# Relative-position softmax: whole-head partitions and chunks of five and six rows in place of one-row tiles

## The chip, the cores and the metric

The kernel runs on one core of a Trainium2 chip. The metric is device time in microseconds (us) of one execution; the time before is a median of 1363.56 us over four runs. The core has a vector engine (DVE), a scalar engine for exponentials (ACT), a general engine that also issues DMAs (GpSimd, called POOL in the profile) and a queue engine (SyncE, SP). Sixteen DMA engines move data between the chip's memory (HBM) and the on-chip memory (SBUF, 128 partitions). The tensor engine isn't used.

## What is computed

Logits of shape 2 x 8 x 2112 x 2112 in float32 get a bias that depends on the head and on the clipped distance between row and column, and then a softmax over the last axis:

```python
B, H, S, _ = logits.shape            # 2, 8, 2112
max_rel = 16
pos = np.arange(S)
rel = pos[:, None] - pos[None, :]
rel_clipped = np.clip(rel, -max_rel, max_rel) + max_rel
bias = rel_bias[:, rel_clipped].copy()        # rel_bias: 8 x 33
logits = logits + bias[None, :, :, :]
logits = logits - logits.max(axis=-1, keepdims=True)
exp = np.exp(logits)
return (exp / exp.sum(axis=-1, keepdims=True)).astype(np.float32)
```

So in each row the bias is one constant to the left of a band of 33 columns around the diagonal, another constant to the right of it, and 33 different values in the band. Input and output are 285.48 MB each; every element is read once and written once. Neither kernel subtracts the row's maximum, which a softmax doesn't need as long as the exponentials stay in range.

## The kernel before

The 33,792 rows of all heads are cut into 264 tiles of 128 consecutive rows; partition p of a tile holds one row of 8448 bytes. A pool `io` of 20 buffers holds the tiles `L`. Per tile:

- SyncE issues the load (line 110).
- DVE adds the band from a template, over 160 columns around the diagonal (line 136). The templates `T` (one per head) and `TP` (for tiles that cross from one head into the next) are made at the start: an extended bias row `e8` is written to a scratch tensor `eD` in HBM, read back shifted by one column per partition (line 65) and copied in reverse order (line 73).
- ACT computes the exponentials in place and sums them, in two instructions where the row has columns to the right of the band: line 143 for the columns up to the band's end, with the left constant as its bias operand, and line 151 for the rest, with the right constant. Templates hold the difference to the left constant. Each has an accumulator read behind it.
- DVE adds the two sums (line 162), takes the reciprocal (line 163) and multiplies the tile by it in place (line 165).
- GpSimd issues the store (line 167).

Loads thus stand on SyncE's queue, with the template loads among the first of them, and stores on GpSimd's. The tile framework allots buffers, places the waits and fixes each engine's order when the program is built; the engines work through their own orders and meet at semaphores. A load that reuses a buffer waits for the store of the tile 20 earlier. On SyncE, a wait for an earlier load on the same semaphore is also placed.

Of the kernel before, what the change touches and what calls it, by code (L numbers as in the profile page):

```python
# [1 line left out]

# [4 lines left out]

FP32 = mybir.dt.float32
EXP = mybir.ActivationFunctionType.Exp  # L10
ADD = mybir.AluOpType.add


@with_exitstack
def kernel(
    ctx: ExitStack,
    tc: tile.TileContext,
    logits: bass.AP,
    rel_bias: bass.AP,
    out: bass.AP,  # L20
):
    nc = tc.nc
    P = 128
    B, H, S, S2 = logits.shape
    assert S == S2
    MR = 16
    W = 2 * MR + 1
    BAND = P + 2 * MR
    EXT = P - 1
    ELEN = 2 * EXT + W  # L30

    logits_f = logits.flatten_outer_dims()
    out_f = out.flatten_outer_dims()
    NR = B * H * S
    assert NR % P == 0
    NT = NR // P

    const = ctx.enter_context(tc.tile_pool(name="const", bufs=1))
    dram = ctx.enter_context(tc.tile_pool(name="dram", bufs=1, space=bass.MemoryType.DRAM))

    rb8 = const.tile([H, W], FP32, tag="rb8")
    nc.sync.dma_start(out=rb8, in_=rel_bias)
    rbB = const.tile([P, H, W], FP32, tag="rbB")
    nc.sync.dma_start(
        out=rbB,
        in_=bass.AP(tensor=rel_bias.tensor, offset=rel_bias.offset, ap=[[0, P], [1, H * W]]),
    )

    e8 = const.tile([H, ELEN], FP32, tag="e8")
    nc.vector.tensor_copy(out=e8[:, 0:EXT], in_=rb8[:, 0:1].to_broadcast([H, EXT]))  # L50
    nc.vector.tensor_copy(out=e8[:, EXT : EXT + W], in_=rb8[:, :])  # L51
    nc.vector.tensor_scalar(  # L52
        out=e8[:, 0 : EXT + W],
        in0=e8[:, 0 : EXT + W],
        scalar1=rb8[:, W - 1 : W],
        scalar2=None,
        op0=mybir.AluOpType.subtract,
    )
    nc.vector.memset(e8[:, EXT + W :], 0.0)  # L59
    eD = dram.tile([H, ELEN], FP32, tag="eD")  # L60
    nc.sync.dma_start(out=eD, in_=e8)

    def load_template(t, p0, np_, h):
        x = const.tile([P, BAND], FP32, tag="X", name="X", bufs=4)
        nc.sync.dma_start(
            out=x[p0 : p0 + np_],
            in_=bass.AP(
                tensor=eD.tensor,
                offset=eD.offset + h * ELEN,
                ap=[[1, np_], [1, BAND]],  # L70
            ),
        )
        nc.vector.tensor_copy(  # L73
            out=t[p0 : p0 + np_],
            in_=bass.AP(
                tensor=x.tensor,
                offset=x.offset + p0 * list(x.ap[0])[0] + (BAND - 1),
                ap=[[list(x.ap[0])[0], np_], [-1, BAND]],
            ),
        )  # L80

    T = []
    for h in range(H):
        t = const.tile([P, BAND], FP32, tag=f"T{h}", name="T")
        load_template(t, 0, P, h)
        T.append(t)
    TP = []
    for k in range(H // 2):
        t = const.tile([P, BAND], FP32, tag=f"TP{k}", name="TP")
        load_template(t, 0, 64, 2 * k)  # L90
        load_template(t, 64, 64, 2 * k + 1)
        TP.append(t)
    io = ctx.enter_context(tc.tile_pool(name="io", bufs=20))
    small = ctx.enter_context(tc.tile_pool(name="small", bufs=16))

    def rb_at(h, k, p0, p1):
        return rbB[p0:p1, h, k : k + 1]

    for t in range(NT):
        rs = P * t  # L100
        f0 = rs // S
        f1 = (rs + P - 1) // S
        if f0 == f1:
            segs = [(0, P, f0, rs - f0 * S)]
        else:
            split = f1 * S - rs
            segs = [(0, split, f0, rs - f0 * S), (split, P, f1, 0)]

        L = io.tile([P, S], FP32, tag="L")
        nc.sync.dma_start(out=L, in_=logits_f[rs : rs + P, :])  # L110

        def seg_ab(p0, p1, i0):
            n = p1 - p0
            c0 = i0 - MR
            return c0, max(c0, 0), min(i0 + n + MR, S)

        max_slots = 1
        for (p0, p1, f, i0) in segs:
            _, _, b = seg_ab(p0, p1, i0)
            max_slots = max(max_slots, 1 + (b < S))  # L120

        s = None
        if max_slots == 2:
            s = small.tile([P, 2], FP32, tag="s", name="s")
        tot = small.tile([P, 1], FP32, tag="tot")

        for (p0, p1, f, i0) in segs:
            h = f % H
            n = p1 - p0
            c0, a, b = seg_ab(p0, p1, i0)  # L130
            nslots = 1 + (b < S)
            if len(segs) == 1:
                tmpl = T[h]
            else:
                tmpl = TP[(f0 % H) // 2]
            nc.vector.tensor_tensor(  # L136
                out=L[p0:p1, a:b],
                in0=L[p0:p1, a:b],
                in1=tmpl[p0 : p0 + n, a - c0 : b - c0],
                op=ADD,  # L140
            )
            acc0 = s[p0:p1, 0:1] if max_slots == 2 else tot[p0:p1, 0:1]
            nc.scalar.activation(  # L143
                out=L[p0:p1, 0:b],
                in_=L[p0:p1, 0:b],
                func=EXP,
                bias=rb_at(h, W - 1, p0, p1),
                accum_out=acc0,
            )
            if nslots == 2:  # L150
                nc.scalar.activation(  # L151
                    out=L[p0:p1, b:S],
                    in_=L[p0:p1, b:S],
                    func=EXP,
                    bias=rb_at(h, 0, p0, p1),
                    accum_out=s[p0:p1, 1:2],
                )
            elif max_slots == 2:
                nc.vector.memset(s[p0:p1, 1:2], 0.0)  # L159

        if max_slots == 2:
            nc.vector.tensor_tensor(out=tot, in0=s[:, 0:1], in1=s[:, 1:2], op=ADD)  # L162
        nc.vector.reciprocal(out=tot, in_=tot)  # L163

        nc.vector.tensor_scalar_mul(out=L[:], in0=L[:], scalar1=tot[:])  # L165

        nc.gpsimd.dma_start(out=out_f[rs : rs + P, :], in_=L[:])  # L167


# [1 line left out]
_INS = ['logits', 'rel_bias']  # L171
_OUTS = [((2, 8, 2112, 2112), 'float32')]


# [23 lines left out]
```

The softmax here doesn't subtract the row's maximum and nothing guards it: scores larger than these inputs give would overflow.

## Time and profile before

| | us |
|---|---|
| median of four runs | 1363.56 (1362.77 to 1364.3) |
| the profiled execution, its time | 1364.13 |
| the profiled execution, its span | 1362.0 |
| ACT busy | 657.5 |
| DVE busy | 518.5 |
| DVE multiply over 128x2112 (line 165), one | 1.320 |
| ACT exponential over 128x2112 (line 143), one | 2.054 |
| accumulator read behind it, one | 0.186 |
| DVE band add over 128x160 (line 136), one | 0.325 |
| DVE reciprocal (line 163), one | 0.164 |
| issue of one store on GpSimd (line 167) | 0.532 |

The span runs from the first to the last event that the profiler recorded; the time of the same execution is 2.1 us more. Busy shares are averages over the whole span. Idle time of an engine costs nothing where another resource sets the pace; which one does is read from the slices, the chain of work that ended last, and the waits. The slices cut the span into 40 equal parts, with a digit for the busy tenths of the mean DMA engine and, below, the GB/s moved.

### The profile page before, as it was taken

What the parts mean: (1) busy time and instruction counts of PE and PEld (TensorE: products, weight loads), DVE (VectorE), ACT (ScalarE), POOL (GpSimd) and SP (SyncE); (2) the same over time, 40 slices, a digit from 0 to 9 for tenths busy, and PEclk for the clock granted to TensorE, in tenths of its full rate; (3) what the DMA queues carried; (4) which work ended last, traced back from release to release, by engine and by line L of the source; (5) the groups of instructions that cost most, each with busy time, mean ns of one, the idle gap of its engine ahead of it and who ended that gap; (6) DMA issues with size and microseconds to landing.
All of it is one profiled execution on the core that took longest, in us unless ns stands there. A gap on an engine that the chain in (4) does not pass through costs nothing.

```text
span 1362.0 us, 3994 instructions
## 1 busy us (share of the span) xinstructions
DVE 518.5 (38%) x1084; ACT 657.5 (48%) x1057; POOL 140.6 (10%) x268
## 2 busy tenths in 40 slices
DVE  3434343343334333334343333433433433333432
ACT  3454444544445444454444544445444454444543
POOL 0011011010101110111011010111101101101100
DMA  8999999999999999999999999999999999999996
GB/s 292 413 428 428 427 427 428 428 426 427 428 428 426 427 428 428 426 427 429 427 426 428 428 427 426 428 428 427 426 428 428 427 426 428 428 427 426 428 428 286
DMA packets 78030, 572.36 MB, mean 420 GB/s; under 512 B 8744, under 2 KB 10416, under 8 KB 10416
## 3 DMA queue, kind: packets, MB, share of 16 engines
q1 hardware_dynamic: 39984, 286.62, 50.3%
q0 software_dynamic: 38016, 285.49, 49.7%
q14 instruction: 30, 0.25, 0.0%
HBM read 286.59 MB, written 285.48 MB: 420 GB/s over the span
## 4 chain that ended last, share of the span: by engine, by line
DMA 98%; issue 1%; DVE 0%; ACT 0%; SPq 0%; POOLq 0%; POOL 0%; ACTq 0%; DVEq 0%
DMA L<-in_logits_dram 96%; DMA X<-eD 1%; DMA eD<-e 0%; ACT L L143 0%; SPq L110 0%; DMA rb<-in_rel_bias_dram 0%; DVE L L165 0%; DVE T L73 0%; POOLq L193 0%; DVE tot L162 0%; POOL out_dram L167 0%; ACT L L151 0%; DVE tot L163 0%; DVE L L136 0%; DVE e L52 0%
## 5 line engine op out<-in xcount | busy, mean ns | idle before, releaser
L151 ACT ACTIVATE L<-L,rbB 128x1968 f32<-128x1968 f32 (+31 forms) x256 | 297.1, 1160 | 655.9 <-DMA L<-in_logits_dram 619.8
L165 DVE TENSOR_SCALAR L<-L,tot 128x2112 f32<-128x2112 f32 x264 | 348.5, 1320 | 8.4
L143 ACT ACTIVATE L<-L,rbB 128x144 f32<-128x144 f32 (+33 forms) x272 | 333.2, 1225 | 29.2 <-DVE L L136 23.8
L167 POOL DMA_DIRECT2D out_dram<-L x264 | 140.4, 532 | 1213.1 <-DVE L L165 1055.3
L136 DVE TENSOR_TENSOR L<-L,T 128x160 f32<-128x160 f32 (+1 forms) x256 | 82.9, 324 | 350.0 <-DMA L<-in_logits_dram 334.6
L162 DVE TENSOR_TENSOR tot<-s 128x1 f32<-128x1 f32 x256 | 40.7, 159 | 423.1 <-ACT L L143 422.5
L163 DVE RECIPROCAL tot<-tot 128x1 f32<-128x1 f32 x264 | 43.3, 164 | 26.3 <-ACT L L143 17.7
L143 ACT ACTIVATION_READ_ACCUMULATOR L<-L,rbB 128x1 f32 (+1 forms) x272 | 50.7, 186 | 0.0
L151 ACT ACTIVATION_READ_ACCUMULATOR L<-L,rbB 128x1 f32 (+1 forms) x256 | 47.6, 186 | 0.0
L136 DVE TENSOR_TENSOR L<-L,TP 64x80 f32<-64x80 f32 x16 | 3.8, 236 | 7.9 <-DMA L<-in_logits_dram 7.7
L73 DVE COPY T<-X 128x160 f32<-128x160 f32 x8 | 1.6, 236 | 12.1 <-DMA X<-eD 12.1
L151 ACT ACT_TABLE_LOAD x1 | 1.3, 1283 | 8.9 <-DMA L<-in_logits_dram 8.9
L73 DVE COPY TP<-X 64x160 f32<-64x160 f32 x8 | 1.9, 238 | 4.7 <-DMA X<-eD 4.6
L50 DVE COPY e<-rb 8x127 f32<-8x127 f32 x1 | 0.2, 213 | 1.2 <-DMA rb<-in_rel_bias_dram 1.2
L59 DVE MEMSET e<- 8x127 f32 x1 | 0.2, 164 | 0.8 <-PEq L182 0.8
L159 DVE MEMSET s<- 64x1 f32 x8 | 0.5, 59 | 0.0
L52 DVE TENSOR_SCALAR e<-e,rb 8x160 f32<-8x160 f32 x1 | 0.3, 292 | 0.0
L51 DVE COPY e<-rb 8x33 f32<-8x33 f32 x1 | 0.2, 160 | 0.0
L182 POOL MEMSET const-float32-0.0<- 128x1 f32 x1 | 0.1, 98 | 0.2 <-issue 0.2
L182 POOL MEMSET const-bfloat16-1.0<- 128x1 bf16 x1 | 0.1, 101 | 0.0
L182 POOL MEMSET const-float32-1.0<- 128x1 f32 x1 | 0.1, 98 | 0.0
L182 POOL MEMSET const-uint8-127<- 128x1 uint8 x1 | 0.1, 98 | 0.0
## 6 DMA issues: line engine op xcount, KB each, us to landing
L<-in_logits_dram SPq DMA_DIRECT2D x264, 1056.0 KB, 40.5
out_dram<-L POOLq DMA_DIRECT2D x264, 1056.0 KB, 13.5
X<-eD SPq DMA_DIRECT2D x8, 80.0 KB, 4.2
X<-eD SPq DMA_DIRECT2D x8, 40.0 KB, 7.6
rbB<-in_rel_bias_dram SPq DMA_DIRECT2D x1, 132.0 KB, 5.2
rb<-in_rel_bias_dram SPq DMA_DIRECT2D x1, 1.0 KB
eD<-e SPq DMA_DIRECT2D x1, 9.0 KB
```

The lines of the kernel that those rows point to most:

```text
L50: nc.vector.tensor_copy(out=e8[:, 0:EXT], in_=rb8[:, 0:1].to_broadcast([H, EXT]))
L52: nc.vector.tensor_scalar(out=e8[:, 0 : EXT + W], in0=e8[:, 0 : EXT + W], scalar1=rb8[:, W - 1 : W], scalar2=None, op0=mybir.AluOpType.sub ...
L73: nc.vector.tensor_copy(out=t[p0 : p0 + np_], in_=bass.AP(tensor=x.tensor, offset=x.offset + p0 * list(x.ap[0])[0] + (BAND - 1), ap=[[list ...
L136: nc.vector.tensor_tensor(out=L[p0:p1, a:b], in0=L[p0:p1, a:b], in1=tmpl[p0 : p0 + n, a - c0 : b - c0], op=ADD,)
L143: nc.scalar.activation(out=L[p0:p1, 0:b], in_=L[p0:p1, 0:b], func=EXP, bias=rb_at(h, W - 1, p0, p1), accum_out=acc0,)
L151: nc.scalar.activation(out=L[p0:p1, b:S], in_=L[p0:p1, b:S], func=EXP, bias=rb_at(h, 0, p0, p1), accum_out=s[p0:p1, 1:2],)
L159: nc.vector.memset(s[p0:p1, 1:2], 0.0)
L162: nc.vector.tensor_tensor(out=tot, in0=s[:, 0:1], in1=s[:, 1:2], op=ADD)
L163: nc.vector.reciprocal(out=tot, in_=tot)
L165: nc.vector.tensor_scalar_mul(out=L[:], in0=L[:], scalar1=tot[:])
L167: nc.gpsimd.dma_start(out=out_f[rs : rs + P, :], in_=L[:])
L182: nc = _bacc.Bacc("TRN2", target_bir_lowering=False, num_devices=1)
```

## The change

Rows are dealt out differently. Two heads have 4224 rows, which is 128 x 33: partition p now owns 33 consecutive rows of a pair of heads, partitions 0 to 63 those of the first head and 64 to 127 those of the second. A chunk takes rows j to j + r of each partition's 33, so in HBM it is one contiguous run of r x 8448 bytes per partition. Chunks alternate between 5 and 6 rows, with smaller ones (1, 2, 4, 6, 4, 6, 4, 6) in the first pair and (5, 6, 5, 6, 4, 3, 2, 1, 1) in the last; there are 53 in all. Buffers are two of 5 rows and two of 6. The first four loads are issued on SyncE ahead of everything else there, the other 49 on GpSimd; all stores are issued on SyncE. A load waits until the store four chunks earlier has landed.

The bias is no longer a band: for each of the four pairs of heads a strip `F` of 2144 columns is built on DVE, in one buffer, from the bias values and from masks that an iota on GpSimd helps to make. Row j of a chunk uses the strip shifted by j columns, so one DVE addition covers up to three whole rows (line 148, over 128x6336). ACT then takes one exponential per row over all 2112 columns with its sum (line 152), DVE one reciprocal for up to three rows (line 153) and one multiply per row (line 156). Templates, scratch tensor and the additions of two partial sums are gone.

In the built program DVE doesn't finish one chunk before the next: for most pairs of chunks the order is both additions of a 6-row chunk, reciprocal and multiplies of its first half, the first addition of the 5-row chunk, then the second half of the 6-row chunk, and so on.

```diff
-    io = ctx.enter_context(tc.tile_pool(name="io", bufs=20))
-    small = ctx.enter_context(tc.tile_pool(name="small", bufs=16))
+    NB = S // W
+    R = 3
+    SLOT = (5, 6)
+    FW = S + W - 1
+    fpool = ctx.enter_context(tc.tile_pool(name="fpool", bufs=1))
+    io = ctx.enter_context(tc.tile_pool(name="io", bufs=2))
+    small = ctx.enter_context(tc.tile_pool(name="small", bufs=8))
+    chunks = []
+    for k in range(H // 2):
+        for b in range(B):
+            sizes = [5, 6] * 3
+            if not chunks:
+                sizes = [1, 2, 4, 6, 4, 6, 4, 6]
+            if k == H // 2 - 1 and b == B - 1:
+                sizes = [5, 6, 5, 6, 4, 3, 2, 1, 1]
+            j = 0
+            for r in sizes:
+                chunks.append((k, (b * H + 2 * k) * S, j, r))
+                j += r
+    def rows(t, row, j, r):
+        return bass.AP(
+            tensor=t.tensor,
+            offset=t.offset + (row + j) * S,
+            ap=[[W * S, P], [1, r * S]],
+        )
+    def load(n, eng):
+        k, row, j, r = chunks[n]
+        size = SLOT[n % 2]
+        L = io.tile([P, size * S], FP32, tag=f"L{size}", name="L")
+        eng.dma_start(out=L[:, 0 : r * S], in_=rows(logits, row, j, r))
+        return L
+    rbB = const.tile([P, H // 2, 2, W], FP32, tag="rbB")
+    nc.scalar.dma_start(
...
+    NPRE = 4
+    pre = [load(n, nc.sync) for n in range(NPRE)]
+    qm = const.tile([P, NB], FP32, tag="qm")
+    for p0 in (0, NB):
+        nc.gpsimd.iota(
+            qm[p0 : p0 + NB],
...
+    for m, op in ((eq, ALU.is_equal), (lt, ALU.is_gt), (gt, ALU.is_lt)):
+        nc.vector.tensor_scalar(out=m, in0=qm, scalar1=0.0, scalar2=None, op0=op)
...
+    def bias_rows(k):
+        F = fpool.tile([P, FW], FP32, tag="F", name="F")
+        low = rbP[:, k, W - 1 : W]
+        high = rbP[:, k, 0:1]
+        rest = small.tile([P, NB], FP32, tag="rest", name="rest", bufs=2)
+        nc.vector.tensor_scalar(out=rest, in0=lt, scalar1=low, scalar2=None, op0=ALU.mult)
+        nc.vector.scalar_tensor_tensor(
+            out=rest, in0=gt, scalar=high, in1=rest, op0=ALU.mult, op1=ALU.add
+        )
...
+        nc.vector.tensor_tensor(out=blocks, in0=wide(eq), in1=rev, op=ALU.mult)
+        nc.vector.tensor_tensor(out=blocks, in0=blocks, in1=wide(rest), op=ALU.add)
+        nc.vector.tensor_copy(out=F[:, 0:MR], in_=low.to_broadcast([P, MR]))
+        nc.vector.tensor_copy(out=F[:, FW - MR : FW], in_=high.to_broadcast([P, MR]))
+        return F
-    for t in range(NT):
...
-        L = io.tile([P, S], FP32, tag="L")
-        nc.sync.dma_start(out=L, in_=logits_f[rs : rs + P, :])
...
-        nc.gpsimd.dma_start(out=out_f[rs : rs + P, :], in_=L[:])
+    F, fk = None, None
+    for n, c in enumerate(chunks):
+        k, row, j, r = c
+        if k != fk:
+            F, fk = bias_rows(k), k
+        L = pre[n] if n < NPRE else load(n, nc.gpsimd)
+        pitch = list(L.ap[0])[0]
+        for s0 in range(0, r, R):
+            w = min(R, r - s0)
+            L3 = bass.AP(
+                tensor=L.tensor, offset=L.offset + s0 * S, ap=[[pitch, P], [S, w], [1, S]]
+            )
+            F3 = bass.AP(
+                tensor=F.tensor,
+                offset=F.offset + W - 1 - j - s0,
+                ap=[[list(F.ap[0])[0], P], [-1, w], [1, S]],
+            )
+            nc.vector.tensor_tensor(out=L3, in0=L3, in1=F3, op=ALU.add)
+            tot = small.tile([P, R], FP32, tag="tot", name="tot")
+            for i in range(w):
+                x = L[:, (s0 + i) * S : (s0 + i + 1) * S]
+                nc.scalar.activation(out=x, in_=x, func=EXP, accum_out=tot[:, i : i + 1])
+            nc.vector.reciprocal(out=tot[:, 0:w], in_=tot[:, 0:w])
+            for i in range(w):
+                x = L[:, (s0 + i) * S : (s0 + i + 1) * S]
+                nc.vector.tensor_scalar_mul(out=x, in0=x, scalar1=tot[:, i : i + 1])
+        nc.sync.dma_start(out=rows(out, row, j, r), in_=L[:, 0 : r * S])
```

## The prediction

> **What bounds the kernel now.** I read the busy table first, then the slices, the chain, the queue table, the waits of the queue that issues the loads, and last the head and the tail in windows.
>
> ```profile
> span 1362.0 us, 3994 instructions
> ...
> DVE 518.5 (38%) x1084; ACT 657.5 (48%) x1057; POOL 140.6 (10%) x268
> ...
> DMA  8999999999999999999999999999999999999996
> GB/s 292 413 428 428 427 427 428 428 426 427 428 428 426 427 428 428 426 427 429 427 426 428 428 427 426 428 428 427 426 428 428 427 426 428 428 427 426 428 428 286
> ...
> q1 hardware_dynamic: 39984, 286.62, 50.3%
> q0 software_dynamic: 38016, 285.49, 49.7%
> ...
> DMA 98%; issue 1%; DVE 0%; ACT 0%; SPq 0%; POOLq 0%; POOL 0%; ACTq 0%; DVEq 0%
> ```
>
> No engine is half busy; the DMA engines are full in 38 of 40 slices, and 98% of the chain is DMA. The two queues' packet times add up to 100% of 16 engines' span. So two things matter: the plateau of 426 to 429 GB/s, and the two slices at the ends.
>
> ```profile
> SPq L110 <- DMA L<-in_logits_dram: 1153.4, 252, 5.4
> ...
> 0.00:20.00 20.00, 6.04 (x20) 8.56 (x13) 1.40 (x6) 1.00 0.78 230
> 20.00:40.00 20.00, 7.82 (x22) 7.28 (x12) 1.59 (x3) 1.00 0.97 370
> ...
> 200.00:600.00 400.00, 152.43 (x317) 196.29 (x315) 41.45 (x78) 1.00 1.01 427
> 600.00:1000.00 400.00, 154.07 (x318) 196.78 (x320) 41.44 (x79) 1.00 1.01 428
> ...
> 1340.00:1350.00 10.00, 3.83 (x8) 4.38 (x7) 1.06 (x2) 1.00 0.61 253
> 1350.00:1356.00 6.00, 1.48 (x2) 1.55 (x2) 0.53 (x1) 1.00 0.73 300
> 1356.00:1362.00 6.00, 0.00 (x0) 0.00 (x0) 0.00 (x0) 1.00 0.18 75
> ```
>
> The first line: each load waits for an earlier load, not for a buffer. The windows (length, busy of DVE, ACT, POOL, clock, DMA share, GB/s) show the plateau and its ends. At 427.5 GB/s (427 from 200 to 600 us, 428 from 600 to 1000) the page's 572.36 MB take 1338.9 us, so 23.1 us of the span are lost: at the head 20 x (1 - 230/427.5) + 20 x (1 - 370/427.5) = 11.9, the remaining 11.2 at the tail.
>
> **What the skill says.** "DMA: Bandwidth & Descriptors", Where 436 GB/s comes from: the ceiling is 16 ports x 32 B x 850 MHz = 435.2 GB/s. Same page, Why small descriptors are slow: some 3 cycles per packet plus 32 B of descriptor data. A row of 8448 B is 264 beats; with 3 + 1 cycles the estimate is 435.2 x 264/268 = 428.7, and the plateau is 427.5: the trace agrees. Same page, Why a DMA increments its semaphore by 16 and not by 1: one descriptor moves one contiguous run of the last dimension. The trace agrees for rows: 33,792 per queue, and with one completion entry for each of the 16 engines per DMA that makes 264 x (128 + 16) = 38,016 packets, as q0 has; longer runs it doesn't show. "SBUF — State Buffer", Who interferes with whom: DVE in a two-port mode, as an fp32 tensor_scalar is, shuts GpSimd out while an instruction lasts, and so its descriptor writing; the trace before can't show it, since each GpSimd DMA there follows the DVE multiply. "VectorE: DVE Perf Modes", The TRN2 errata: an fp32 tensor_tensor takes (N + 151)/0.96 ns; for 160 that is 324, and the band add measured 325.
>
> **The change, part by part.**
>
> *Transfer rate.* Loads and stores go from 128 runs of 8448 B to 128 runs of 5 or 6 rows (42 to 51 KB). If a run stays one packet, the four cycles are paid once for 5.5 rows: 1452 beats + 4, and one cycle more for a share of the completion entry (one per engine and DMA, beside eight data packets), so 435.2 x 1452/1457 = 433.7 GB/s (estimate from the page, fitted to the plateau). Bounds: 427.5 (runs are cut again) and 435.2. I take 433.7. Bytes: 2 x 285.48 MB + 0.13 for the bias + up to 0.25 of instruction fetch = 571.35 MB, so 1317.4 us (1336.5 and 1312.8 at the bounds). The 16 template loads and the scratch round trip go.
>
> *Head.* Before, the first logits load is third on SP at 1.60 us and moved bytes reach the plateau at 6 us; templates then break the stream (dips to 86 and 125 GB/s at 16 to 18 us). After, loads of 1, 2, 4 and 6 rows head the SP queue, 13 rows or 32 us of traffic, with nothing between. By 7 us before had moved 1.125 MB: 4.4 us lost. I take 4 lost. These loads hide the bias build: bias vector landed at about 5.5 us (it took 5.2 before, now on ACT's queue), two tensor_tensor over 2112 at 2.36 us and some ten small DVE operations at 0.2: strip ready at about 12 us, first add 2.4, exp 2.2, multiply 1.3, first store issued near 21 us, the next two (2 and 4 rows) near 27 and 45. The fifth load waits for the first store to land, about 28 us, and the four preloads last until 44 with these stores beside them. By the same count of rows the strip may slip to about 25 us before the DMA runs dry; the iotas on GpSimd that feed it, and a library load the built program puts ahead of them, are unpriced by the trace. I put them under 13 us, so the cost is nothing; a slip beyond costs one for one.
>
> *Compute.* Adds: 264 rows x 2112/0.96 ns = 580.8 us, plus 100 instructions x 0.157 = 596. Multiplies stay 348.5. Reciprocals 100 x 0.164 = 16 (43.3 before); sum of two accumulators (40.7) and band adds (82.9) go. Four strips at 5.7: 23. DVE: 985 us, 75% of 1317. ACT: 264 x (2.054 + 0.186) = 591, from the row of 128x2112 and its accumulator read. Both stay below the DMA time, but no longer far below, and order now counts.
>
> *Buffers and waits.* 20 tiles of one row become four of 5, 6, 5, 6 rows; a load waits for the store four chunks back, on GpSimd, where only loads stand. At 433.7 GB/s a chunk of 5.5 rows costs 13.7 us each way, so a period of 27.4 and a turn of 109.7. The built program's DVE order puts the first add of chunk B (5 rows) ahead of the second half of chunk A (6 rows), so A's end waits for B's landing. With both queues at half rate (5.0 us a row): A lands at 0, its two adds take 13.5; B lands at 24.9, add to 31.7, then B's second add 36.4, A's last multiplies 40.4: store at 41, B's at 48. For half of the head pairs the order delays stores to about 50 after landing. Turn: 27.4 load + 50 + 27.4 store = 105, leaving 5 us of 110, of which landing and issue take 2 to 3 (an estimate: the last store before was issued at 1353.4 and its data moved by 1357.3). A load later than that doesn't idle the engines while stores are queued: alone, loads reached 423 to 448 GB/s at 6 to 8 us, and stores alone 406 at 1355 to 1357. Idle needs both queues empty. The longest stretch from a landing to the next store is 16 to 20 us; standing against it are two loads, 27 us. I take nothing, with 7 to 11 us to spare per pair.
>
> *GpSimd's loads, SP's stores.* 49 loads replace 264 stores on GpSimd (0.53 us each there). A load's descriptors can be held behind a run of up to six multiplies, 7.9 us. It is covered by the store queue; below zero it can't go, above it is the slow rival.
>
> *Tail.* Last chunks are 4, 3, 2, 1, 1 rows. Counting rows by hand from the last 6-row landing, the final one-row load lands with three stores, 6 rows or 15 us, still queued; its add, exp and multiply (6.5 us) fit under them. After the last data 4.7 us passed before the end; that stays. 2 us for uneven engines: before, the load at 1343 to 1347 crept at 84 GB/s with a fifth of the engines busy.
>
> *Sum.* 1317.4 + 4 + 4.7 + 2 = 1328.1 as a span. The profiled run took 1364.13 with a span of 1362.0, so 2.1 lie around it, and the median shown is 0.6 lower: 1329.6, rounded to 1330.
>
> **Rivals.**
>
> 1. *The runs are cut again*, or per-row cost isn't per packet: plateau stays 427.5, only the ends gain. 1336.5 + 10.7 + 1.5 = 1349. For it: the trace has one large packet size only, so no measured slope. Against: the overhead fits so well.
>
> 2. *The strip is late.* At 35 us instead of 12, 10 us beyond the slack: 1340. For: an untimed GpSimd library load. Against: 13 us of slack.
>
> 3. *Slower: GpSimd's loads are held by DVE.* DVE is at 75% with two-port multiplies in rows of three to six. A hold of 7.9 plus a landing of 2.6 against a mean margin of 9 leaves 1.5 us of empty engines per chunk: 53 x 1.5 = 80, so 1410. It decides from (1366 - 1330)/53 = 0.7 us a chunk. For: four buffers, 5 us of slack in the late order. Against: holds are rarely longest, and stores usually stand in the other queue.
>
> **Numbers.** Forecast 0.58, rival 1 0.17, rival 2 0.06, rival 3 0.15, and 0.04 for something near no change. A measurement here can't tell less than 0.2%, 2.7 us. Faster 0.81, same 0.04, slower 0.15. The range goes from 1322 (435.2 GB/s, ends a little better) to 1358 (rival 1 with a 10 us slip), leaving out rival 3 and no change.
>
> **What would show it.** A plateau of 432 to 435 GB/s in the slices and packets of 42 KB and more (53 x 2 x 144, some 15,000 packets in all, where 78,030 were) prove the rate step; 427 to 428 with full slices is rival 1. A first slice near 380 proves the head; a dip in slices 2 and 3 is rival 2. DVE should read 960 to 1000 us, ACT 560 to 595. DMA share falling to 8 or 9 tenths throughout, with loads late behind GpSimd issues while DVE multiplies, is rival 3 and would make the forecast wrong.

## The result and the profile after

The changed kernel took 1358.68 us (median of 35 runs, 1350.5 to 1371.0) against 1363.49 for the kernel before (55 runs, 1362.1 to 1365.3). The ratio is 0.9963, with a 95% interval of 0.9954 to 0.9972: faster by 0.4%, where 2.5% was forecast, and 0.7 us above the range. Ratios, here and below, leave out runs more than 1.5% above the fastest of their kernel (one here, one in e6, one in e7); medians and ranges keep them. The profiled execution took 1356.79 us with a span of 1355.0. Its page, first the busy times, the slices and the packets:

```profile
span 1355.0 us, 1475 instructions
...
DVE 949.5 (70%) x493; ACT 524.6 (39%) x529; POOL 33.1 (2%) x55
...
DMA  9999999999999999999999999999999999999988
GB/s 395 422 432 431 434 429 427 434 432 434 430 392 434 433 431 424 438 423 435 435 395 400 426 428 428 418 433 427 441 432 423 407 435 426 432 403 436 423 350 353
DMA packets 15420, 571.18 MB, mean 422 GB/s; under 512 B 1713, under 2 KB 1841, under 8 KB 1841
```

Packets fell from 78,030 to 15,420, so a run of 5 or 6 rows is one packet. Good slices move 430 to 441 GB/s, above the 428 of before. But the row is no longer flat: it has holes of 392, 395, 400, 407 and 403, and two weak slices at the end. Before had no holes, and one weak slice at its end. The chain and the queue's waits say the same:

```profile
DMA 68%; DVE 23%; another core or an unknown queue 6%; issue 2%; ACT 1%; POOL 0%; POOLq 0%; ACTq 0%
...
L68 POOL DMA_DIRECT2D L<-in_logits_dram x49 | 32.5, 664 | 1296.4 <-DMA out_dram<-L 994.1
```

DMA held 98% of the chain before; now DVE has 23%. The second line is GpSimd's row: 49 load issues, 664 ns each, and 994 us of waiting for a store to land. Before, loads waited for loads; now they wait for buffers. Four windows (length, busy of DVE, ACT, POOL, clock, DMA share, GB/s) split the loss:

```profile
0.00:33.90 33.90, 23.80 (x23) 7.34 (x7) 0.55 (x6) 1.00 0.96 395
33.90:67.80 33.90, 30.05 (x15) 19.79 (x20) 1.81 (x2) 1.00 1.01 423
67.80:1287.20 1219.40, 857.56 (x430) 477.63 (x483) 28.56 (x44) 1.00 1.00 426
1287.20:1355.00 67.80, 38.06 (x28) 19.87 (x20) 2.15 (x3) 1.00 0.84 352
```

At the forecast rate of 433.7 GB/s, 571.18 MB take 1317.0 us, 38.0 less than the span. Each window's length times (1 - rate/433.7) says where these are: 3.9 in the first two slices, 21.6 in the middle, 12.8 in the last two (rounding adds 0.3).

One hole from close by, first the timeline of DVE, SP's queue and GpSimd at the start of the second pair of heads (start, length, engine and line, operation; in brackets the idle time before and what ended it):

```profile
356.43 6.76 DVE L148 TENSOR_TENSOR L<-L,F 128x6336 f32<-128x6336 f32 x1 [17.01 <-DMA L<-in_logits_dram]
...
363.25 6.74 DVE L148 TENSOR_TENSOR L<-L,F 128x6336 f32<-128x6336 f32 x1
369.90 6.23 DVE L156 TENSOR_SCALAR L<-L,tot 128x2112 f32<-128x2112 f32 x5
...
376.16 17.80 SPq L157 DMA_DIRECT2D out_dram<-L  x2
376.93 0.53 POOL L68 DMA_DIRECT2D L<-in_logits_dram  x1 [27.54 <-DMA out_dram<-L]
379.46 6.76 DVE L148 TENSOR_TENSOR L<-L,F 128x6336 f32<-128x6336 f32 x1 [3.19 <-DMA L<-in_logits_dram]
```

and the DMA in windows of the same stretch:

```profile
366.00:374.00 8.00, 8.00 (x5) 7.15 (x9) 0.00 (x0) 1.00 0.97 419
374.00:376.00 2.00, 2.00 (x2) 2.00 (x3) 0.00 (x0) 1.00 0.31 131
376.00:380.00 4.00, 0.81 (x4) 0.03 (x1) 0.53 (x1) 1.00 0.85 348
380.00:382.00 2.00, 2.00 (x1) 0.00 (x0) 0.00 (x0) 1.00 1.60 549
382.00:384.00 2.00, 2.00 (x1) 0.00 (x0) 0.00 (x0) 1.00 0.59 177
```

A chunk had landed at 328.1. DVE then stood idle for 17 us (the bracket of the first line) and waited for the next chunk, because the chunk's five multiplies come later in its order: they stand behind the additions of the chunk that landed at 356.4. So the store is issued at 376.16, 48 us after landing. The store before had landed at 376.4 and freed a buffer for the load at 376.93. So around 375 the engines had nearly nothing: the one load under way and the one store both were finishing. By the profile's record of single packets, five of the 16 engines had one at 376.0, and the first packet of the new load came at 382.2, 5.2 us after its issue began. Windows this short book a whole packet where it starts (hence 549), so they are read together: from 374 to 384 the mean is 311 GB/s.

The profile also records every DMA packet, with its start, duration and size, but not which engine moved it. These records divide the loss of the middle window. At no moment of it is there no load under way, and only for 2 us no store. Engines without a packet add up to 6.5 us of all 16 engines. Packets of 42,240 and 50,688 B took 1561 and 1872 ns at the median, but 374 of 11,334 took over a tenth longer, up to 3.6 us, and what they took beyond the median adds up to 14.4 us of all 16. In e4 (a copy without compute) and e2 (seven smaller buffers) below, whose middle has no holes, these sums are 0.0 and 0.4, and 0.0 and 0.5 us. So idle engines are about a third of this loss; the rest are busy engines with packets that last longer. Why these last longer stays open.

### The profile page after: what moved, and what is told of

Same layout as the page of the kernel before. It is cut to its first block, busy times and chain, and to the rows that moved or that the text cites. A ratio compares the mean times of both kernels' runs of the same rounds, so it can differ in the third digit from the quotient of the medians.

```text
span 1355.0 us, 1475 instructions
## 1 busy us (share of the span) xinstructions
DVE 949.5 (70%) x493; ACT 524.6 (39%) x529; POOL 33.1 (2%) x55
## 2 busy tenths in 40 slices
DMA packets 15420, 571.18 MB, mean 422 GB/s; under 512 B 1713, under 2 KB 1841, under 8 KB 1841
## 4 chain that ended last, share of the span: by engine, by line
DMA 68%; DVE 23%; another core or an unknown queue 6%; issue 2%; ACT 1%; POOL 0%; POOLq 0%; ACTq 0%
DMA L<-in_logits_dram 40%; DMA out_dram<-L 28%; DVE L L148 14%; DVE L L156 8%; ACT L L152 1%; DMA rbB<-in_rel_bias_dram 1%; DVE F L125 0%; DVE F L124 0%; DVE tot L153 0%; POOL L L68 0%; POOLq L68 0%; DVE rest L104 0%; DVE rest L105 0%; DVE rbP L96 0%
## 5 line engine op out<-in xcount | busy, mean ns | idle before, releaser
L148 DVE TENSOR_TENSOR L<-L,F 128x6336 f32<-128x6336 f32 (+1 forms) x100 | 594.2, 5958 | 380.5 <-DMA L<-in_logits_dram 374.6
L152 ACT ACTIVATE L<-L 128x2112 f32<-128x2112 f32 x264 | 515.2, 1952 | 816.2 <-DVE L L148 559.4
L156 DVE TENSOR_SCALAR L<-L,tot 128x2112 f32<-128x2112 f32 x264 | 332.5, 1315 | 1.4
L68 POOL DMA_DIRECT2D L<-in_logits_dram x49 | 32.5, 664 | 1296.4 <-DMA out_dram<-L 994.1
L152 ACT ACTIVATION_READ_ACCUMULATOR L<-L 128x1 f32 x264 | 49.3, 187 | 0.0
L153 DVE RECIPROCAL tot<-tot 128x3 f32<-128x3 f32 (+1 forms) x100 | 15.7, 164 | 10.7 <-ACT L L152 10.7
L124 DVE TENSOR_TENSOR F<-eq,rbP 128x2112 f32<-128x2112 f32 x4 | 9.4, 2356 | 0.0
L125 DVE TENSOR_TENSOR F<-F,rest 128x2112 f32<-128x2112 f32 x4 | 9.4, 2351 | 0.0
```

Source lines behind the costliest of these rows:

```text
L68: eng.dma_start(out=L[:, 0 : r * S], in_=rows(logits, row, j, r))
L124: nc.vector.tensor_tensor(out=blocks, in0=wide(eq), in1=rev, op=ALU.mult)
L125: nc.vector.tensor_tensor(out=blocks, in0=blocks, in1=wide(rest), op=ALU.add)
L148: nc.vector.tensor_tensor(out=L3, in0=L3, in1=F3, op=ALU.add)
L152: nc.scalar.activation(out=x, in_=x, func=EXP, accum_out=tot[:, i : i + 1])
L153: nc.vector.reciprocal(out=tot[:, 0:w], in_=tot[:, 0:w])
```

## The experiments

Two theories stood at first. A: with four large buffers and an interleaved DVE order both queues run empty. B: the long packets are slow themselves.

For each DMA the trace has its issue and the moments at which the 16 engines report. From these, means over the chunks (without the first 8 and last 9), in us: hold is landing to store issue; spread is first to last engine of one DMA, loads and stores; lead is how long before a landing the next load was issued; the turn is landing to landing of one buffer, and its floor is the bytes of a turn at the plateau's rate. (e8, which compute bounds, isn't listed.)

| kernel | hold | spread | lead | turn (floor) | time |
|---|---|---|---|---|---|
| the changed kernel | 36.9 | 4.2, 6.6 | 5.7 | 111.8 (109.7) | 1358.7 |
| e1, chunks in order | 21.7 | 7.2, 11.0 | 12.0 | 111.1 (109.7) | 1342.1 |
| e3, one-row packets | 36.4 | 2.6, 2.4 | 7.1 | 111.4 (111.2) | 1350.0 |
| e5, both | 21.7 | 3.6, 1.4 | 22.5 | 111.2 (111.2) | 1345.0 |
| e4, copy alone | 0.0 | 5.0, 2.1 | 30.2 | 110.2 (109.7) | 1328.7 |
| e6, queues exchanged | 37.4 | 4.0, 5.3 | 5.1 | 111.3 (109.7) | 1353.2 |
| e2, seven of 3 rows | 38.9 | 2.9, 2.7 | 16.2 | 105.3 (105.0) | 1331.3 |
| e9, five of 3 rows | 31.7 | 2.2, 2.0 | 5.0 | 76.6 (75.0) | 1359.1 |
| e7, four of 3 rows | 26.0 | 1.8, 2.6 | 2.7 | 61.9 (60.0) | 1389.7 |

### e1: DVE finishes each chunk before the next

```diff
+            with ExitStack() as st:
+                if prev is not None:
+                    st.enter_context(tc.issue_after(prev))
                 nc.vector.tensor_tensor(out=L3, in0=L3, in1=F3, op=ALU.add)
...
         nc.sync.dma_start(out=rows(out, row, j, r), in_=L[:, 0 : r * S])
+        prev = last.ins
```

Here `last` is the chunk's last multiply.

> Only DVE's order changes: every chunk's last multiply stands ahead of the next chunk's first addition, so a store no longer waits for the next landing. Theory A (four large buffers and the interleaved DVE order let both queues run empty): stores leave about 23 us after landing, the slices at 392 to 407 GB/s go, 1338 to 1348 us against 1358.7. Theory B (packets of 42 to 51 KB are themselves slow at every hand-over, whatever the order): 1355 to 1361.

Measured: 1342.1 us, ratio 0.9845 (0.9831 to 0.9858), as theory A said. The hold fell by 15 us and the holes went:

```profile
GB/s 398 411 433 437 426 433 432 437 437 430 434 434 427 433 432 435 432 428 433 436 428 435 424 434 432 433 433 432 429 430 435 433 428 430 434 423 436 412 391 275
```

No slice of the middle is below 423. The end is worse than the changed kernel's, though, with 391 and 275 (a slice is 33.6 us), and the engines' spread grew to 7 and 11 us.

### e2: seven buffers of 3 rows

```diff
-    SLOT = (5, 6)
+    SLOT = (3,)
-    io = ctx.enter_context(tc.tile_pool(name="io", bufs=2))
+    io = ctx.enter_context(tc.tile_pool(name="io", bufs=7))
-            sizes = [5, 6] * 3
+            sizes = [3] * 11
...
-    NPRE = 4
+    NPRE = 7
```

(The first pair begins with 1, 2; the last ends with 1, 1, 1.)

> Chunks of 3 rows in seven buffers (177 KB, 186 KB in the changed kernel), so several loads and stores can stand in the queues; everything else stays. Theory A: all dry spells go, plateau 432 to 433 GB/s, 1328 to 1337 us. Theory B: packets are half as long, so half the loss goes, 1343 to 1350.

Measured: 1331.29 us, within 0.16 us in four runs, ratio 0.9766 (0.9753 to 0.9779). This beats both kernels, with less SBUF. The edit changes the number of buffers and the length of chunks together; e7 and e9 below keep the length and change the number. Its slices:

```profile
GB/s 388 430 432 431 434 431 435 430 435 431 434 431 433 432 433 432 433 432 432 434 431 433 432 432 432 431 435 431 434 432 434 432 432 433 432 432 433 432 431 369
```

The reader should see a plateau at 432 to 433 that no longer has a hole, though the hold of 38.9 us is longer than the changed kernel's: there is room for it. The rate is also what the prediction's sum gives for 3 rows: 435.2 x 792/797 = 432.5.

### e3: one-row packets, all else unchanged

```diff
-            ap=[[W * S, P], [1, r * S]],
+            ap=[[W * S, P], [S, r], [1, S]],
...
-        L = io.tile([P, size * S], FP32, tag=f"L{size}", name="L")
+        L = io.tile([P, size, SP], FP32, tag=f"L{size}", name="L")
```

`SP` is S + 8, so rows aren't adjacent on chip.

> Chunks of 5 and 6 rows in the same four buffers and order, but rows stand 32 bytes apart on chip, so that each packet is one row of 8448 B again. Theory A: the dry spells stay and the plateau falls to 427.5 GB/s, 1372 to 1380 us. Theory B: the slow long packets go, 1340 to 1350.

Measured: 1349.96 us, ratio 0.9902 (0.9889 to 0.9916). Theory A as stated fell: it said 1372 to 1380, and the result is the upper edge of theory B's range. The plateau did drop to 428, and yet the kernel won 8.7 us, because the holes became shallower:

```profile
GB/s 380 414 428 428 428 428 428 428 429 428 429 412 428 420 428 427 428 429 428 428 429 408 427 423 429 429 428 428 429 428 428 410 429 423 427 428 429 429 422 373
```

They stand where they stood (slices 12, 22, 32), at 408 to 412 in place of 392 to 407. The spread of stores is 2.4 in place of 6.6 us. So B had a part: long packets do cost something where buffers are tight. Theory A became, as an argument still to be tested: the hold, and the time by which the engines of one long-packet DMA finish apart, together exceed what four buffers allow.

### e4: copy alone

All compute between load and store is left out.

> All compute is left out: each chunk is loaded and stored again unchanged, with the same chunks, buffers and queues. Theory A: a store follows its landing at once, queues stay full, 1323 to 1331 us. Theory B: the slow packets stay, 1340 to 1350.

Measured: 1328.67 us. Long packets with no hold run at 433 to 434 GB/s through the middle:

```profile
200.00:600.00 400.00, 0.00 (x0) 7.39 (x14) 1.00 1.00 433
600.00:1000.00 400.00, 0.00 (x0) 7.91 (x15) 1.00 1.00 434
1000.00:1300.00 300.00, 0.00 (x0) 5.81 (x11) 1.00 1.00 433
```

So packets of 42 to 51 KB aren't slow in themselves, and the rate of the forecast is there to be had.

### e5: in order and one-row packets

The diffs of e1 and e3 together.

> Both edits together: DVE finishes each chunk in turn, and packets are one row of 8448 B; four buffers of 5 and 6 rows stay. If what runs the queues dry is the sum of a long hold in the buffer and of engines that finish a long-packet DMA far apart (6 to 11 us for stores in the in-order kernel, 2.4 with one-row packets), both are gone and only the rate is lower: 571.2 MB at 427.5 GB/s, plus 9 at the ends and 2 around the span, 1344 to 1350 us. If order alone was the cause and short packets only cost rate, 1342 + 19 = 1361.

Measured: 1344.99 us, ratio 0.9864 (0.9852 to 0.9877), the number of the combined theory. Its windows:

```profile
200.00:600.00 400.00, 289.39 (x141) 157.61 (x159) 12.83 (x15) 1.00 1.01 428
600.00:1000.00 400.00, 288.03 (x148) 158.60 (x162) 11.98 (x14) 1.00 1.01 428
1000.00:1300.00 300.00, 215.43 (x107) 116.57 (x118) 9.09 (x11) 1.00 1.01 428
1300.00:1343.00 43.00, 22.58 (x15) 14.06 (x14) 1.09 (x2) 1.00 0.90 378
```

The middle is flat at its lower rate, and the last 43 us move 378 GB/s, where e1 with long packets had 281 in the same stretch:

```profile
1300.00:1343.30 43.30, 20.05 (x15) 14.06 (x14) 1.06 (x2) 1.00 0.68 281
```

So long packets earn some 19 us in rate (1336.1 against 1317.0), and with DVE in order they give back 16 of them at the end and to a less full middle: e1 is only 2.9 us ahead of e5.

### e6: queues exchanged

```diff
-        L = pre[n] if n < NPRE else load(n, nc.gpsimd)
+        L = pre[n] if n < NPRE else load(n, nc.sync)
...
-        nc.sync.dma_start(out=rows(out, row, j, r), in_=L[:, 0 : r * S])
+        nc.gpsimd.dma_start(out=rows(out, row, j, r), in_=L[:, 0 : r * S])
```

> The changed kernel with its queues exchanged: all loads on SyncE, stores on GpSimd. The prediction's slow rival (loads on GpSimd are held while DVE multiplies): 1335 to 1345 us. The theory of hold and skew, to which the issuing engine doesn't matter: 1352 to 1364, with the same dips.

Measured: median 1353.15 us, but 1345.8 to 1369.1 over six runs, ratio 0.9918 (0.9887 to 0.995). The median lies in the range for hold and spread, but without the highest run it is 1349.5, in neither range; the rival's range is missed by all runs, by the fastest narrowly. The holes stay (375 and 366 GB/s in slices 9 and 12 of its profile, an execution of 1361.0 us), and hold, spread and lead are nearly those of the changed kernel. A few us may hang on the queue: from the issue of a load to its first packet it is 3.9 us at the median here, 4.8 in the changed kernel. The scatter doesn't settle it. The changed kernel's own trace is the better witness against held loads: from a store's landing to the load's issue it is 0.57 us, and an issue takes 664 ns, 132 more than before.

### e7 and e9: four and five buffers of 3 rows

`bufs` and `NPRE` of e2 at 4 and 5.

> Chunks of 3 rows with four buffers in place of seven. Theory of turns: four buffers give 60 us at full rate, and load 15, hold 20 to 39, store 15 and some 6 of skew need 56 to 75, so the queues run dry: 1370 to 1450 us. If packet length alone decided, 1331 to 1340 as with seven.

> Five buffers of 3 rows, a turn of 75 us at full rate, between four (60 us, 1390) and seven (105 us, 1331). Theory of turns: load 18, hold 26 to 39, store 17 and the skew that these contain need 62 to 75, so nearly all dry spells go: 1331 to 1342 us. If cost fell evenly with each buffer: (1390 - 1331)/3 per buffer, 1370.

Measured: 1389.7 us with four (1385.8 to 1408.0), ratio 1.0237 (1.0187 to 1.0286), as the turns said. With five 1359.12 (1350.4 to 1366.2), ratio 0.9969 (0.9952 to 0.9986): a miss for both forecasts, nearer to an even fall with each buffer (1370) than to the theory of turns (1331 to 1342). The turn was 76.6 against a floor of 75.0, and the lead of loads 5.0 us, that of the changed kernel. Times line up with the lead: 2.7 us gives 1390, 5 to 6 give 1359, 16 gives 1331. In e9 the DVE order also changed when the program was built (some stretches finish a chunk before the next), so it isn't a pure change of number, and part of its loss may be what e8 shows.

### e8: seven buffers, in order

The diffs of e1 and e2 together.

> Seven buffers of 3 rows, and DVE finishes each chunk in turn. If order matters only where the turn of a buffer is tight, it changes nothing here: 1329 to 1333 us as with the interleaved order. If interleaving costs by itself, some of the 16 us that it cost with four buffers is won: 1315 to 1326.

Measured: 1495.4 us, ratio 1.0966 (1.0951 to 1.0981), which neither said. With one addition per chunk, in order means that DVE waits for ACT and ACT for DVE:

```profile
599.73 6.75 DVE L152 TENSOR_TENSOR L<-L,F 128x6336 f32<-128x6336 f32 x1
...
612.55 0.18 DVE L157 RECIPROCAL tot<-tot 128x3 f32<-128x3 f32 x1 [6.06 <-ACT L L156]
612.76 3.78 DVE L160 TENSOR_SCALAR L<-L,tot 128x2112 f32<-128x2112 f32 x3
...
616.45 6.75 DVE L152 TENSOR_TENSOR L<-L,F 128x6336 f32<-128x6336 f32 x1
```

From one addition to the next it is 16.7 us: add 6.8, wait for three exponentials 6.1, multiplies 3.8. Three rows cost the DMA 15.0, so the compute chain became the bound: 264 rows are 88 times that, 1470 us. In e1 a chunk has two halves, so one half's exponentials lie beside the other half's addition. The interleaved order of the changed kernel is thus not a fault in itself: with one addition per chunk some overlap between chunks is needed, and with four large buffers this overlap is costly.

## Why the prediction was wrong

- *Bound and rate: right.* The best slices, e4's 433 to 434 and e2's 432 to 433 against 432.5 from the same sum bear out the four cycles per packet that the prediction worked out from the Trainium skill's page "DMA: Bandwidth & Descriptors" (Where 436 GB/s comes from, and Why small descriptors are slow; the page has 3 cycles and 32 B), which the kernel before could show for one size only.
- *Head: right.* 4 us were put there, 3.9 were lost. The strip was ready at 13.9 us (12 forecast), the first three stores left at 22.2, 27.6 and 45.7 (21, 27, 45). The iotas were done at 1.2 us; rival 2 is out.
- *Compute: right where it mattered.* DVE 949.5 (985 forecast; 960 to 1000 named), ACT 524.6 (591; 560 to 595 named): both were over-priced and lie outside what was named, since consecutive instructions overlap (264 multiplies of 1315 ns were busy 332.5 us, not 347) and the exponential over 2112 took 1952 ns, not 2054. (The parts given for DVE add up to 983.5, not 985.)
- *Buffers and waits: wrong, and here most of the 2.5% went.* The step that failed is "Idle needs both queues empty", and with it "standing against it are two loads, 27 us" and "I take nothing, with 7 to 11 us to spare per pair". The middle lost 21.6 us with a load under way all the time and a store for all but 2 us. The hold was forecast well (stores at 41 to 50 us after landing for the chunks that wait; measured over the table's chunks 41 at the median, 48 at the 90th percentile). But the sum 27.4 + 50 + 27.4, with 2 to 3 for landing and issue, took a DMA to start soon after its issue and to end at once on all engines (only the tail has 2 us for uneven engines), and no load to wait behind the one ahead. Measured, it is 0.6 us from a store's landing to the next load's issue, and from there 4.8 us at the median, never under 4.3, to that load's first packet (35 loads). From issue to landing a load took 33.6 and a store 40.7 us; with a mean hold of 36.9 and the 0.6 that is the turn of 111.8 against 109.7. Loads were issued only 5.7 us ahead of the previous landing, and the engines of one DMA ended 4.2 to 6.6 us apart, so an engine that was early had no next load yet. A single load, nearly done, stood against the stretch, not two. e1 (hold) and e3 (packets) each removed part of the loss, e5 nearly all of it at the lower rate; e2 made room and removed the holes altogether. That the spread itself, and not some other property of long packets, is what e3 removed was not isolated.
- *Tail: right but for one more hole, and in part by luck.* 6.7 us were put there, 12.8 lost. By the sum used above, 5.7 of these fell in a hole of the middle's kind, at 1288 to 1296 us:

```profile
1288.00:1292.00 4.00, 4.00 (x4) 3.92 (x5) 0.00 (x0) 1.00 0.41 175
1292.00:1296.00 4.00, 3.75 (x6) 1.09 (x2) 1.09 (x1) 1.00 0.42 76
```

The other 7.1 are near the forecast, but two of its parts missed in opposite directions. I counted three stores, 6 rows, queued behind the last landing, and there were two, 3 rows, since loads waited for stores one by one. What follows the last data shrank from 4.7 to 1.6 us (the last packet ended at 1353.4).

- *Rivals.* Rival 1 (runs cut again, or a cost by row) is refuted by the packet count and by e4's 433 GB/s. Rival 3 named the right place, too little slack in four buffers, with the wrong cause: GpSimd's issue was hardly held. The Trainium skill's page "SBUF — State Buffer" (Who interferes with whom) allows such a hold; here an issue took 0.13 us more than before, and a load started 0.9 us later than on SyncE's queue in e6, whatever the reason. The time lies only 0.7 us above the range by chance: the upper end stood for rival 1 with a late strip, and neither came.

## What to carry to other kernels

In a kernel bound by DMA, work out a buffer's whole turn: issue to first packet, wait behind the DMA ahead, transfer at half rate, hold, store, until the slowest engine has finished, and compare it with buffers times bytes at full rate. A turn that just fits was too long here. What told the kernels with holes from those without was the lead of the next load, set against the time from a load's issue to its first packet plus the spread of loads. In us, the sum is 4.8 + 4.2 = 9.0 against a lead of 5.7 in the changed kernel, 7.9 against 5.1 in e6, 7.3 against 7.1 in e3, 6.7 against 5.0 in e9 and 6.4 against 2.7 in e7, all with holes; it is 11.6 against 12.0 in e1 and 7.4 against 16.2 in e2, without (e4 and e5, also without, have leads of 30.2 and 22.5). (The first part is the median of the loads whose first packet can be told, in e1 the shortest, as most of its loads wait behind another; in e2 only one could be told.) This comparison was found afterwards, and no run tested it.

More, smaller buffers can beat fewer, larger ones: seven of 3 rows did (1331), five didn't (1359, as the changed kernel). From packets of 25 KB to those of 5.5 rows the rate gains only 0.3% (432.5 to 433.7 GB/s by the sum that fitted).

## What the runs showed of the hardware

- From the issue of a load on GpSimd to its first packet it was 4.3 us or more in the changed kernel (median 4.8), also where the loads' queue was empty (e9, 4.5, 12 loads); on SyncE 3.9 in e6. The first load of the changed kernel, issued on SyncE before anything else moved, had its first packet after 1.0 us.
- In kernels with holes, packets of one size took up to twice as long as their median in the changed kernel and up to three times in e9, and this cost more than idle engines did: 14.4 against 6.5 us in the changed kernel's middle, 21.5 against 5.6 in e9's, 0.5 against 0.0 in e2's.
- The time scattered from 1350 to 1371 us for the changed kernel and from 1350 to 1366 for e9, both with holes, and within 0.16 us for e2. But e4, without holes, went from 1326.5 to 1335.0, so holes aren't the only source of scatter.
- Engines of one DMA can finish further apart with long packets: stores 11.0 us in e1 against 1.4 in e5, the same order with one-row packets. Length alone doesn't do it: in e4 stores of long packets ended 2.1 us apart.
